# Aggregating neighbours on one core: second-pass steps regrouped over the slots, and half of the first pass's spreading given to GpSimd

## The chip, the cores and the metric

One core of one Trainium2 chip runs the kernel. The metric is the device time of the program in microseconds; each kernel is executed many times and the median is compared. A profile is one execution taken with the hardware profiler.

## The reference

```python
num_nodes, num_edges, dim = 4096, 65536, 128
for i in range(len(edge_index_src)):
    output[edge_index_dst[i]] += node_features[edge_index_src[i]]
```

Every edge adds the 128 features of its source node to its destination node. Source and destination are random integers below 4096, the features are float32, and the output is 4096 x 128 float32.

## The kernel before

**The idea.** Nodes are numbered in 32 blocks of 128. The sum over edges becomes matrix products, if the edges are first sorted by source block and by destination block. The kernel sorts them on the chip in two passes. A pass gives each edge a rank (a count of the earlier edges in its bucket), builds a one-hot permutation matrix from the ranks, and moves the edges with a matmul on TensorE. At the end each slot (one of 32) builds, for its destination block, count matrices between blocks of nodes, and multiplies the features with them.

**Engines and order.** The order of the instructions on every engine is written out by hand: each engine runs its own queue in the order in which the code emits it, and waits on semaphores for the others. The letters in the code are V (VectorE, DVE in the profile), S (ScalarE, ACT), G (GpSimd, POOL) and PE (TensorE).

**First pass, six quads (`for q in range(NQ)`).** A quad is four columns of edges. For quad q, `oh1s` (V) compares the destination blocks with an iota that lies in PSUM, `counts` (PE and S) makes the ranks, and `spread1` (line 262) multiplies the one-hot by two keys. It fills the tile `v1[q]`, whose two halves k=0 (key `ka`, the node codes) and k=1 (key `kb`, the source blocks) are one V instruction each, 128 x 2816. `move1` then builds the permutation `p` on V (line 201, the helper `onehot`) and runs the matmuls `psm` (line 286) with `v1` as the moving operand. `v1` has two buffers, tags A0 and A1, so quad q+1's tile is free when quad q-1's matmuls have been done. While quads 2 to 5 are moved, `beside` counts group 0 of the second pass: `buckets0` (V), a product `vc` on G (line 361), and `ranks0`. `clear` (line 149) zeroes the permutation tiles `p2a` and `p2c` with four GpSimd memsets each. `x_part` (lines 186 and 190) splits the features in two parts, on S and G.

**Second pass, groups 0 to 5 with 4, 4, 4, 4, 8, 8 columns (`pass2`).** Each group is a list of steps; a step is a V part, a PE part and a part for two slots later. The steps of a group of four are: `buckets4` (line 596) with its `payloads` on G (line 535, six products) and the column sums; `sums_to_each` (V) with `counts_ranks` (PE, S, line 622 and on); two pairs of `permutations` (V, four one-hots of line 201 into `p2a` or `p2c`) and `permuted` (PE, line 581). After the second pair of a quad of columns, `quad_keys` makes the keys `slo` and `dlo` (line 412, V). A group of eight has: `buckets` (line 520), 32 short compares on V, one for each source block, then `before_all` (PE, line 528); `running` (line 547), eleven dependent additions on V, whose results G multiplies in `masked` (line 552, twelve products), and behind them in G's queue twelve `payloads`; `ranks` (PE, line 560); four pairs. G's products are appended to a list and handed out by `little`, but on G they simply stand in that order.

**The slots.** Slot n issues on V: the keys that are due, `onehots(n+1)` (two instructions of 128 x 4096), then the V parts of the slot's steps. On PE it issues: the 32 matmuls of `blocks(n)` (`psa`, line 657) and the 16 of `product` for slot n-1 (`pso`, line 664) in two halves, then the PE parts of the steps. `onehots` has two buffers, so `onehots(n+1)` waits for the blocks of slot n-1. `STEPS` says which groups make a step in which slot:

```python
STEPS = {0: (1, 2), 1: (1,), 2: (2,), 3: (3,), 4: (2,), 5: (3, 2), 6: (4,), 7: (4,), 8: (3,),
         9: (3,), 10: (4,), 12: (4,), 13: (4,), 14: (5,), 15: (5,), 16: (4,), 17: (4,), 18: (5,),
         20: (5,), 21: (5,), 24: (5,), 25: (5,)}
```

Group 1's first two steps stand ahead of the loop, around `onehots(0)`. Slot 4's one-hots need the keys of group 1, slot 8's those of group 2, and so on; slots 16 to 23 use group 4, and slots 24 to 31 group 5.

Of the kernel before, what the change touches and what calls it, by code (L numbers as in the profile page):

```python
# [8 lines left out]
P = 128  # L9
# [5 lines left out]
OP = mybir.AluOpType  # L15
AX = mybir.AxisListType

NB = 32
NCH = 24
NJ = 22  # L20
NH = NCH // 2
NQ = NCH // 4
# [2 lines left out]
BIG = 4096.0  # L25
GROUPS = (4, 4, 4, 4, 8, 8)

STEPS = {0: (1, 2), 1: (1,), 2: (2,), 3: (3,), 4: (2,), 5: (3, 2), 6: (4,), 7: (4,), 8: (3,),
         9: (3,), 10: (4,), 12: (4,), 13: (4,), 14: (5,), 15: (5,), 16: (4,), 17: (4,), 18: (5,),
         20: (5,), 21: (5,), 24: (5,), 25: (5,)}  # L30


WIN = ((0, 7, 0, 64), (7, 14, 4, 100), (14, NJ, 20, P))
# [3 lines left out]
def kernel(  # L37
# [32 lines left out]
    with ExitStack() as fast:  # L70
        fast.enter_context(tc.manual_schedule())
        _fast(fast, tc, node_features, src32, dst32, out, ident, fmax, flag_i, T)
# [6 lines left out]
def _fast(ctx, tc, X, src32, dst32, out, ident, fmax, flag_i, T):  # L79
    nc = tc.nc  # L80
    V, S, G, PE = nc.vector, nc.scalar, nc.gpsimd, nc.tensor
# [62 lines left out]
    p2a = sb1.tile([P, 2, NCH, P], BF16, name="p2a")  # L144

    def clear(t):
        for i in range(2):
            for h in range(2):
                G.memset(t[:, i, h * NH:(h + 1) * NH, (1 - h) * 64:(2 - h) * 64], 0.0)


    NL = NJ * 4
# [3 lines left out]
    kb = sb1.tile([P, NQ, NL, 2], BF16, name="kb", tag="K1")  # L156
    ka = sb1.tile([P, NQ, NL, 2], U16, name="ka", tag="K2")
    kab = ka[:].bitcast(BF16)
# [24 lines left out]
    def x_part(i, v):  # L183
        blks = slice(i % 2 * BX, (i % 2 + 1) * BX)
        if v == 0:
            S.copy(out=xr[i // 2][:, blks, 0, :], in_=xf[i])  # L186
        else:
            for h in range(2):
                bs = slice(i % 2 * BX + h * BX // 2, i % 2 * BX + (h + 1) * BX // 2)
                G.tensor_tensor(out=xr[i // 2][:, bs, 1, :], op=OP.subtract,  # L190
                                in0=xf[i][:, h * BX // 2:(h + 1) * BX // 2],
                                in1=xr[i // 2][:, bs, 0, :])
# [3 lines left out]
    oh1, sums, rank1, v1 = {}, {}, {}, {}  # L196
# [9 lines left out]
    def oh1q(q):  # L206
        return oh1[q // 2][:, q % 2]

    def oh1s(q):

        if q % 2 == 0:
            oh1[q // 2] = sb1.tile([P, 2, NL, NB], BF16, name="oh1", tag=f"o{q // 2}")
        onehot(oh1q(q), kd[:, q], NL, NB)
        pst = ps.tile([P, 512], F32, name="pst", tag=("ps2", "pso")[q % 2], bufs=1)
        for j in range(NJ):
            PE.matmul(out=pst[:, j:j + 1],  # L216
                      lhsT=oh1q(q)[:, 4 * j:4 * j + 4, :].rearrange("p l b -> p (l b)"),
                      rhs=ones[:, :1], start=True, stop=True)
        sums[q] = pst
# [32 lines left out]
    def count(q, n=99):  # L252
        for _ in range(n):
            next(counting[q], None)
# [2 lines left out]

    def spread1(q):

        v1[q] = sb1.tile([P, NL, 2, NB], BF16, name="v1", tag=f"A{q % 2}")  # L260
        for k, key in ((0, kab), (1, kb[:])):
            V.tensor_tensor(  # L262
                out=v1[q][:, :, k, :].rearrange("p t (b k) -> p t b k", k=2),
                in0=oh1q(q).rearrange("p t (b k) -> p t b k", k=2),
                in1=key[:, q, :, None, :].to_broadcast([P, NL, NB // 2, 2]), op=OP.mult)


    def place(q):
# [7 lines left out]
    def move1(q, meanwhile):  # L276
        psm = ps.tile([P, 512], F32, name="psm", tag="misc", bufs=1)
        for l in range(4):
            t = p1[l // 2]
            n = len([j for j in range(NJ) if j * NCH + q * 4 + l < T])  # L280
            for j0, j1, m0, m1 in WIN:
                j1 = min(j1, n)
                onehot(t[:, l % 2, j0:j1, m0:m1], rank1[q][:, l, j0:j1], j1 - j0, m1 - m0, m0=m0)
            meanwhile(l)
            for j in range(n):
                PE.matmul(out=psm[:, l * 64:(l + 1) * 64], lhsT=t[:, l % 2, j, :],  # L286
                          rhs=v1[q][:, 4 * j + l].rearrange("p k b -> p (k b)"),
                          start=j == 0, stop=j == n - 1)
        pv = psm[:, :256].rearrange("p (l k b) -> p l k b", l=4, k=2)
        S.copy(out=sa[:, place(q), :], in_=pv[:, :, 0, :])  # L290
        S.copy(out=sbk[:, place(q), :], in_=pv[:, :, 1, :])
# [37 lines left out]
    x_part(2, 1)  # L329
    count(0)  # L330
    spread1(0)
    scan(2)
    count(1, 2)
# [1 line left out]
    count(1)  # L335
    x_part(3, 0)
    x_part(3, 1)
    clear(p2a)


    keys2 = {}
# [73 lines left out]
    def most_rank(g, r):  # L415
        V.tensor_reduce(out=fmax[:, g:g + 1], in_=r[:, :, :, 0], op=OP.max, axis=AX.XY)
# [39 lines left out]
    def during(q):  # L456

        def step(l):
            beside(q, l)
            if l == 0:  # L460
                if q + 2 < NQ and q == 0:
                    count(2, 2)
                return
            if l == 1:
                if q + 3 < NQ:
                    scan(q + 3)
            if q + 2 < NQ:
                count(q + 2, 2)
        return step

    for q in range(NQ):
        if q == NQ - 1:
            p2c = sb1.tile([P, 2, NCH, P], BF16, name="p2c", tag="o2")
            clear(p2c)
            p2b += [p2c[:, 0], p2c[:, 1]]
        move1(q, during(q))
        if q + 2 < NQ:
            count(q + 2)
        if q + 4 < NQ:
            oh1s(q + 4)  # L480
        if q + 1 < NQ:
            spread1(q + 1)
# [13 lines left out]
    def pass2(g):  # L496
# [9 lines left out]
        def flat2(t):  # L506
            return t.rearrange("p c i s k -> p c (i s k)")

        def tiles():
            at = -(g - 1) % 3  # L510
            tags = ("c0", "o1", "o0")
            T2["o"] = sb1.tile(shape, BF16, name="oh2", tag=tags[at])[:]
            T2["c"] = sb1.tile(shape, BF16, name="cum2", tag=tags[(at + 1) % 3])[:]
            T2["v"] = sb1.tile(shape, BF16, name="v2", tag="F" if g % 2 == 0 else "c1")[:]

        def buckets():
            tiles()
            ds = slice(d0, d0 + gd)
            for s in range(NB):
                V.tensor_single_scalar(  # L520
                    out=T2["o"][:, :, :, s, :], scalar=float(s + 1), op=OP.is_equal,
                    in_=sbk[:, :, ds].rearrange("p c (i k) -> p c i k", k=kk))
# [17 lines left out]
                for c in range(0, NCH, 4):  # L540
                    small.append(((g, 1), lambda i=i, c=c: payload(i, slice(c, c + 4))))

        def running():
            cums = flat2(T2["c"]).rearrange("p (h c) w -> p h c w", h=2)
            ohs2 = flat2(T2["o"]).rearrange("p (h c) w -> p h c w", h=2)
            for c in range(1, NH):
                V.tensor_tensor(out=cums[:, :, c], in0=cums[:, :, c - 1], in1=ohs2[:, :, c - 1],  # L547
                                op=OP.add)

# [79 lines left out]
        pairs = []  # L629
# [5 lines left out]
        def both(*fs):  # L635
            return lambda: [f() for f in fs]

        if gd == 4:
            return [(both(buckets4, payloads), column_sums), (sums_to_each, counts_ranks)] + pairs
        return [(buckets, before_all), (both(running, masked, payloads),),  # L640
                (lambda: None, ranks)] + pairs


    def onehots(slot):

        oh = sb1.tile([P, 2, 4 * 8, P], BF16, name="oh", tag=f"t2{slot % 2}")
        at = slot % 4 * 32
        n = 16 if slot == 0 else 32
        for i in range(0, 32, n):
            for k, io in ((0, piotas), (1, piota)):  # L650
                onehot(oh[:, k, i:i + n], keys2[slot // 4][k][:, at + i:at + i + n], n, io=io)
        return oh
# [14 lines left out]
    def flag():  # L667
# [13 lines left out]
                               op=OP.not_equal)  # L681

    todo = [[]] + [pass2(g) for g in range(1, len(GROUPS))]

    def run(fs):
# [8 lines left out]
    for cs in done0:  # L694
        permute0((2, 3), cs)
    nvec, nmat = todo[1].pop(0)
    nvec1, nmat1 = todo[1].pop(0)
    nvec()
    ranks0(last0)
    permuted0((2, 3), done0, 0)  # L700
# [8 lines left out]
    nmat()  # L709
    put_keys(0, pa0)  # L710
    oh = onehots(0)
    nvec1()
    nmat1()
    most_rank(0, T0["r"])
    slots = NB
    prev, pso = None, None
# [1 line left out]
    for slot in range(slots):  # L718
        for f in late.pop(slot, ()):
            f()  # L720
        steps = [todo[g].pop(0) for g in STEPS.get(slot, ())]
        late[slot + 2] = [f for st in steps for f in st[2:]]
# [117 lines left out]
```

## Time and profile before

| what | value |
|---|---|
| median of 14 runs | 341.77 us (340.58 to 342.87) |
| the profiled execution | 341.12 us, its span 339.5 us |
| TensorE, weight loads | 292.4 us (86%), 245.3 us (72%) |
| VectorE | 286.0 us (84%) in 385 instructions |
| ScalarE | 195.2 us (58%) |
| GpSimd | 99.8 us (29%) in 109 instructions |
| mean granted TensorE clock | 0.951 |

The span runs from the first to the last instruction. The profile's page gives each engine's busy time, the span in 40 equal slices (8.5 us each) with the busy tenths of each engine, the chain of waits that ended last, and groups of instructions by line with the mean of one. Further views are the waits by engine, tables of stretches of time, and the timeline of one engine, in which equal neighbours are merged into one row. Starts in the timeline are in us from the span's start.

### The profile page before, as it was taken

The numbers are of one execution on the slowest core, as the hardware profiler recorded it, in microseconds if no ns is written. First come the engines' busy times: TensorE is split into PE (matmuls) and PEld (weight loads), VectorE is DVE, ScalarE is ACT, GpSimd is POOL, SyncE is SP. The second block draws the span as 40 slices with busy tenths as digits, with TensorE's granted clock in tenths as the row PEclk, the third lists the DMA queues.
The fourth block names the chain that finished last, engine by engine and source line by source line (L and its number), as shares of the span: only waits on it lengthen the run. The fifth ranks groups of instructions, "written<-read, shape, count | busy, mean of one in ns | idle before, by whom it ended". The sixth has DMA issues, their size and how long they took to land.

```text
span 339.5 us, 8887 instructions
## 1 busy us (share of the span) xinstructions
PE 292.4 (86%) x3880; PEld 245.3 (72%) x3880; DVE 286.0 (84%) x385; ACT 195.2 (58%) x395; POOL 99.8 (29%) x109
## 2 busy tenths in 40 slices
PE   0679798577389899899699999987999999999994
PEld 0468676576178688688588888866888888888883
DVE  4999999976969939958999899999989959958800
ACT  2766546211175856855555666572656676677761
POOL 6637021142507070003998000189910000000000
PEclk9999979967599999999979999997999999999998
DMA  8500000000000000100001001000100100100101
GB/s 240 131 2 5 2 3 2 2 4 2 1 2 3 2 0 2 33 3 0 2 2 31 2 3 33 0 2 0 34 2 2 33 0 2 33 0 3 33 2 31
DMA packets 8712, 5.82 MB, mean 17 GB/s; under 512 B 224, under 2 KB 8416, under 8 KB 8672
## 3 DMA queue, kind: packets, MB, share of 16 engines
q1 hardware_dynamic: 8528, 4.72, 5.1%
q10 hardware_dynamic: 144, 0.52, 0.6%
q8 instruction: 30, 0.49, 0.6%
q14 instruction: 10, 0.08, 0.1%
HBM read 3.15 MB, written 2.10 MB: 15 GB/s over the span
## 4 chain that ended last, share of the span: by engine, by line
PE 61%; DVE 26%; ACT 6%; issue 5%; DMA 2%; DVEq 0%; ACTq 0%
PE pso L664 30%; PE psa L657 15%; DVE oh L201 7%; PE ps L581 7%; DVE p L201 6%; DVE v L262 5%; DVE cum L547 5%; PE psr L560 3%; ACT cum L625 2%; DMA raw<-in_edge_index_dst_dram 2%; ACT a L659 1%; PE psx L305 1%; PE pst L390 1%; PE psm L286 1%; PE ps L404 1%
## 5 line engine op out<-in xcount | busy, mean ns | idle before, releaser
L659 ACT CAST a<-psa 128x512 fp32r<-128x512 f32 x256 | 131.6, 604 | 47.0 <-PE psa L657 46.9
L664 PE MATMUL pso<-a,xr 128*128 128x512 f32 x512 | 133.5, 403 | 0.0
L664 PEld LDWEIGHTS pso<-a,xr 128*128 128x128 f32 x512 | 91.6, 189 | 16.9
L201 DVE TENSOR_TENSOR oh<-psi,slo 128x4096 bf16<-128x4096 uint16 (+1 forms) x33 | 73.2, 2219 | 21.7 <-PE psa L657 21.3
L201 DVE TENSOR_TENSOR oh<-psi,dlo 128x4096 bf16<-128x4096 uint16 (+1 forms) x33 | 73.1, 2214 | 0.0
L657 PE MATMUL psa<-oh 128*128 128x128 bf16 x1024 | 70.1, 222 | 0.4
L657 PEld LDWEIGHTS <-oh 128*128 128x128 bf16 x1024 | 59.5, 99 | 12.0 <-issue 11.7
L535 POOL TENSOR_TENSOR v<-oh,sa 128x512 bf16<-128x512 bf16 x42 | 42.6, 1047 | 35.9 <-DVE oh L596 24.5
L552 POOL TENSOR_TENSOR cum<-cum,oh 128x512 bf16<-128x512 bf16 x24 | 29.5, 1249 | 68.0 <-DVE cum L547 34.6
L201 DVE TENSOR_TENSOR p<-psi,rank 128x448 bf16<-128x448 uint16 (+3 forms) x72 | 29.7, 470 | 0.0
L241 ACT ACTIVATE cum<-psc,minus 128x512 bf16<-128x512 f32 (+1 forms) x36 | 21.4, 655 | 11.6 <-PE psc L238 11.3
L286 PE MATMUL psm<-v,p 128*128 128x64 bf16 x512 | 21.1, 199 | 2.0 <-DVE p L201 1.8
L286 PEld LDWEIGHTS <-p 128*128 128x128 bf16 x512 | 18.9, 102 | 2.7 <-DVE p L201 2.4
L201 DVE TENSOR_TENSOR p2a<-psi,rank 128x768 bf16<-128x768 uint16 (+2 forms) x36 | 15.9, 502 | 2.6 <-ACT rank L565 2.6
L581 PE MATMUL ps<-v,p2a 128*128 128x32 bf16 x336 | 12.2, 195 | 6.2 <-DVE p2a L201 6.2
L547 DVE TENSOR_TENSOR cum<-cum,oh 128x512 bf16<-128x512 bf16 x22 | 16.1, 731 | 1.5 <-ACT cum L531 0.8
L625 ACT ACTIVATE cum<-psc,minus 128x512 bf16<-128x512 f32 x18 | 11.2, 693 | 10.6 <-PE psc L622 8.7
L581 PEld LDWEIGHTS <-p2a 128*128 128x128 bf16 x336 | 11.2, 103 | 8.3 <-DVE p2a L201 7.1
L201 DVE TENSOR_TENSOR p2c<-psi,rank 128x768 bf16<-128x768 uint16 (+2 forms) x36 | 15.8, 500 | 0.0
L190 POOL TENSOR_TENSOR xr<-xf,xr 128x512 fp32r<-128x512 f32 x8 | 11.8, 1496 | 13.2 <-ACT xr L186 13.2
L216 PE MATMUL pst<-ones,oh 128*128 128x1 bf16 x132 | 4.3, 164 | 12.2 <-DVE oh L201 12.2
L234 PE MATMUL psc<-oh,early 128*128 128x512 bf16 (+1 forms) x36 | 14.7, 408 | 0.0
(97 smaller groups left out, 290.1 us busy)
## 6 DMA issues: line engine op xcount, KB each, us to landing
xf<-in_node_features_dram SPq DMA_DIRECT2D x4, 512.0 KB, 7.5
out_dram<-rows SPq DMA_DIRECT2D x8, 256.0 KB, 2.3
raw<-in_edge_index_src_dram ACTq DMA_DIRECT2D x1, 512.0 KB, 5.0
raw<-in_edge_index_dst_dram SPq DMA_DIRECT2D x1, 512.0 KB, 5.2
```

Of the source, the lines that this page charges most:

```text
L201: V.tensor_tensor(out=dst.rearrange("p i (m k) -> p i m k", k=2), in0=io.rearrange("p i (m k) -> p i m k", k=2), in1=keys2[:, :, None, :]. ...
L241: S.activation(out=cum[:, :, 4 * j0:4 * (j0 + n)], func=RELU, bias=minus[:], in_=psc[:, :n * P].rearrange("p (t b) -> p b t", b=NB))
L262: V.tensor_tensor(out=v1[q][:, :, k, :].rearrange("p t (b k) -> p t b k", k=2), in0=oh1q(q).rearrange("p t (b k) -> p t b k", k=2), in1=ke ...
L286: PE.matmul(out=psm[:, l * 64:(l + 1) * 64], lhsT=t[:, l % 2, j, :], rhs=v1[q][:, 4 * j + l].rearrange("p k b -> p (k b)"), start=j == 0, ...
L535: G.tensor_tensor(out=T2["v"][:, cs, i], in0=T2["o"][:, cs, i], op=OP.mult, in1=sa[:, cs, None, ds].to_broadcast([P, cs.stop - cs.start, N ...
L547: V.tensor_tensor(out=cums[:, :, c], in0=cums[:, :, c - 1], in1=ohs2[:, :, c - 1], op=OP.add)
L552: small.append(((g, 0), lambda c=c: G.tensor_tensor(out=flat2(T2["c"])[:, c:c + 2], in0=flat2(T2["c"])[:, c:c + 2], in1=flat2(T2["o"])[:, ...
L581: PE.matmul(out=ps2[:, d % 4 * NB:(d % 4 + 1) * NB], lhsT=p2b[d % 4][:, c, :], rhs=T2["v"][:, c, d // kk, :, d % kk], start=c == 0, stop=c ...
L625: S.activation(out=flat2(T2["c"])[:, c0:c0 + 4].rearrange("p c w -> p (c w)"), in_=psc[:], func=RELU, bias=minus[:])
L657: PE.matmul(out=psa[:, i * P:(i + 1) * P], lhsT=oh[:, 0, 4 * k + i, :], rhs=oh[:, 1, 4 * k + i, :], start=True, stop=True)
L659: S.copy(out=a[:, k, :], in_=psa[:])
L664: PE.matmul(out=pso[:], lhsT=xr[s // 16][:, s % 16, v, :], rhs=a[:, k, :], start=s == 0 and v == 0, stop=s == NB - 1 and v == 1)
```

## The change

Three things are changed. First, `spread1` of quads 1 to 5 keeps only the half `ka` on VectorE; the half `kb` of quad q+1 is made by GpSimd in four pieces of 128 x 704, put into its queue at the start of quad q's move. `clear(p2a)` moves from ahead of the loop to behind the pieces of quad 2. Quad 0 is still spread by VectorE alone. Second, the second step of group 1 moves from ahead of the slots into slot 0. Third, a group of eight has ten steps and not seven: its 32 compares are made in two halves of 16, `before_all` is a step of its own, and `running` is made in two parts of five and six additions. `STEPS` is rewritten to spread these.

```diff
-STEPS = {0: (1, 2), 1: (1,), 2: (2,), 3: (3,), 4: (2,), 5: (3, 2), 6: (4,), 7: (4,), 8: (3,),
-         9: (3,), 10: (4,), 12: (4,), 13: (4,), 14: (5,), 15: (5,), 16: (4,), 17: (4,), 18: (5,),
-         20: (5,), 21: (5,), 24: (5,), 25: (5,)}
+STEPS = {0: (1, 2), 1: (1, 1), 2: (2, 3), 3: (4,), 4: (2, 3), 5: (2,), 6: (4, 4), 7: (4,),
+         8: (3, 4), 9: (3,), 10: (4, 5), 11: (5,), 12: (4,), 13: (4, 5), 14: (5,), 15: (5,),
+         16: (4,), 17: (4,), 18: (5,), 20: (5,), 21: (5,), 24: (5,), 25: (5,)}
...
     def spread1(q):
+        if q == 0:
+            new_v1(q)
+            times_key(V, q, 1, 0, NL)
+        times_key(V, q, 0, 0, NL)
+
+    def new_v1(q):
         v1[q] = sb1.tile([P, NL, 2, NB], BF16, name="v1", tag=f"A{q % 2}")
-        for k, key in ((0, kab), (1, kb[:])):
-            V.tensor_tensor(
-                out=v1[q][:, :, k, :].rearrange("p t (b k) -> p t b k", k=2),
-                in0=oh1q(q).rearrange("p t (b k) -> p t b k", k=2),
-                in1=key[:, q, :, None, :].to_broadcast([P, NL, NB // 2, 2]), op=OP.mult)
+
+    def times_key(e, q, k, t0, t1):
+        e.tensor_tensor(
+            out=v1[q][:, t0:t1, k, :].rearrange("p t (b k) -> p t b k", k=2),
+            in0=oh1q(q)[:, t0:t1].rearrange("p t (b k) -> p t b k", k=2),
+            in1=(kab, kb[:])[k][:, q, t0:t1, None, :].to_broadcast([P, t1 - t0, NB // 2, 2]),
+            op=OP.mult)
...
     x_part(3, 1)
-    clear(p2a)
...
     for q in range(NQ):
+        if q + 1 < NQ:
+
+            new_v1(q + 1)
+            for t0 in range(0, NL, NL // 4):
+                times_key(G, q + 1, 1, t0, t0 + NL // 4)
+        if q == 1:
+            clear(p2a)
...
-        def buckets():
-            tiles()
+        def buckets(h):
+            if h == 0:
+                tiles()
             ds = slice(d0, d0 + gd)
-            for s in range(NB):
+            for s in range(h * NB // 2, (h + 1) * NB // 2):
...
-        def running():
+        def running(c0, c1):
...
-            for c in range(1, NH):
+            for c in range(c0, c1):
...
-        return [(buckets, before_all), (both(running, masked, payloads),),
-                (lambda: None, ranks)] + pairs
+        wait = lambda: None
+        return [(lambda: buckets(0),), (lambda: buckets(1),), (wait, before_all),
+                (lambda: running(1, 6),),
+                (both(lambda: running(6, NH), masked, payloads),),
+                (wait, ranks)] + pairs
...
     nvec, nmat = todo[1].pop(0)
-    nvec1, nmat1 = todo[1].pop(0)
...
     oh = onehots(0)
-    nvec1()
-    nmat1()
     most_rank(0, T0["r"])
```

## The prediction

> **What bounds the kernel now.** I read the page's busy slices and its chain first, then a table of stretches, TensorE's waits, and the timelines of VectorE and GpSimd.
>
> ```profile
> DVE  4999999976969939958999899999989959958800
> ...
> PE 61%; DVE 26%; ACT 6%; issue 5%; DMA 2%; DVEq 0%; ACTq 0%
> ...
> 20.00:30.00 10.00, 8.18 (x170) 6.91 (x169) 10.00 (x17) 7.55 (x16) 4.38 (x4) 1.00 0.01 2
> ...
> 84.00:98.00 14.00, 7.39 (x94) 5.41 (x92) 11.33 (x12) 4.39 (x9) 5.13 (x6) 0.61 0.00 1
> ...
> 231.50:300.00 68.50, 68.50 (x806) 58.30 (x807) 60.56 (x51) 43.76 (x88) 15.97 (x16) 0.98 0.05 13
> ...
> PE ps L581 <- DVE p2a L201: 6.2, 2, 3.3
> ...
> PE psc L622 <- DVE sums L612: 5.8, 1, 5.8
> ```
>
> The stretches list PE, PEld, DVE, ACT, POOL, clock, DMA. The chain gives TensorE 61% and VectorE 26% of the span. From 14 to 68 us VectorE is full and sets the pace; between 84 and 98 us neither engine is full; from 98 us on TensorE is full, but for two holes of 3.3 us (first wait row), after the eleven additions of groups 4 and 5. So the change has three places to gain: VectorE's half `kb` in the first pass, the 5.8 us at the slots' start, and the two holes. What it costs shows only in the timelines:
>
> ```profile
> 27.31 3.88 POOL L190 TENSOR_TENSOR xr<-xf,xr 128x512 fp32r<-128x512 f32 x2 [5.62 <-ACT xr L186]
> ...
> 27.41 2.66 DVE L262 TENSOR_TENSOR v<-oh,ka 128x2816 bf16<-128x2816 bf16 x1
> ...
> 156.53 8.40 DVE L547 TENSOR_TENSOR cum<-cum,oh 128x512 bf16<-128x512 bf16 x11 [0.84 <-ACT cum L531]
> ...
> 173.73 12.11 POOL L535 TENSOR_TENSOR v<-oh,sa 128x512 bf16<-128x512 bf16 x12
> ...
> 181.75 4.25 DVE L412 TENSOR_SCALAR slo<-pa 128x256 uint16<-128x256 uint16 x1
> 185.92 0.28 DVE L412 TENSOR_SCALAR dlo<-pa 128x256 uint16<-128x256 uint16 x1
> ...
> 209.32 3.90 DVE L520 TENSOR_SCALAR oh<-sbk 128x192 bf16<-128x192 bf16 x32
> ```
>
> `ka` takes 1.61 us alone but 2.66 beside GpSimd's first product; `slo` takes 0.28 alone but 4.25 while the twelve payloads end (185.84). The one-hots of line 201, which read an iota in PSUM and one tile in SBUF, take 2.28 beside GpSimd and 2.28 without. So VectorE's products of two SBUF tiles and its compares and shifts wait for GpSimd, and GpSimd for them. At 27.41, 84.41 and 85.08 VectorE got in after one GpSimd instruction; at 181.75 only when GpSimd's queue was empty.
>
> The Trainium skill ("SBUF — State Buffer", SBUF: two separate sides) has one port pair for both, held for a whole instruction by whoever starts first. By that `slo` would have waited for one payload, 1.04 us, and not for four; the row shows more than the rule. It speaks against this change either way.
>
> **First pass.** VectorE loses five `kb` halves: 10.7 us for six (1788 ns each) less 1.61 for quad 0, so 9.1 us of a full engine. GpSimd gets 20 pieces of 704. The nearest row is the payload, with the same types and a second operand repeated along the free dimension: 1.01 us from start to start for 512. With memsets' 0.03 us of fixed cost a piece is 1.38. The masked product of plain operands, 1.12 for 512, would make it 1.53. No row of two inputs is cheaper than the payload's. I take 1.38, 5.5 us a quad. GpSimd's queue then holds, without a gap from 27.3 us on: two `x_part` products 2.5, 20 pieces 27.6, `clear(p2a)` 2.7, three `vc` 3.1, and five `ka` of VectorE that lock it out, 5 x 1.55 = 7.8. Sum 43.7, so quad 5's `kb` is ready at 71.0. Before, quad 5's matmuls began at 71.6, behind `ranks0`. VectorE itself would be at quad 5's permutation only 1 us earlier than before, since at each quad it waits for TensorE's matmuls, which wait for GpSimd's pieces (quad 1: ready at 36.7, needed at 31.2). And behind `kb` stand `vc`, `clear(p2c)` and another `vc`, 1.05 + 2.75 + 1.05: at 75.9 the last product for `permuted0`, which began at 75.95 before. So the 9.1 us come to nothing: I take 0; the range goes from -1 (VectorE's lead) to +3 us (20 pieces at 1.53). GpSimd becomes the bound here.
>
> By the Trainium skill ("GPSIMD Engine Reference", Elementwise — side-by-side cycle accounting), 2.6 cycles an element at 1.2 GHz, a piece would be an estimated 1.53 us and this term 3 us instead of 0.
>
> **Slots 0 to 6.** Before, TensorE waited 5.8 us for group 1's scans (90.88), did its ranks until 97.4, then blocks(0), `permuted` (1.5) and group 2's column sums; slot 1's blocks began at 102.34. Now blocks(0) fill the hole (88.5 to 92.5), but the scans are queued behind `onehots(1)`: 90.95 + 4.4 = 95.4. The ranks take 5.6 (115.12 to 120.73, full clock) to 6.5 (90.88 to 97.4, half), column sums 0.6. Slot 1 starts at 95.6 + 6.0 + 0.6 = 102.2, as before, but with 1.5 us of `permuted` still to do. That is +1.4 us, and it stays, because TensorE is full from there on. `buckets4` of group 3 and the first 16 compares of group 4 (1.9) come to slots where VectorE waits for TensorE anyway (5.1 us before 124.67). Slot 7 starts at 156.8 instead of 155.43.
>
> **Slots 7 to 10.** A slot of TensorE is 5.63 us (109.48 to 115.12), plus 1.52 for `permuted`, 2.53 for `before_all`, 2.67 for group 4's `ranks`, 0.39 where results are transposed. VectorE has 4.4 for two one-hots, 1.85 for four of `permutations`. The additions are 0.46 each, but 1.3 where GpSimd's masked product holds it. The eleven (8.4) become 3.15 + 4.45. Running sum: additions start 1.1 us after slot 7's start, at 157.9; to 161.05; onehots(9) to 165.45; permutations to 167.3; additions to 171.75; onehots(10) to 176.15; permutations. TensorE: slot 7 to 162.4, slot 8 to 168.1, `permuted` to 169.6, slot 9 to 175.6, and then it waits; the last permuted block ends 2.38 after the permutations start (169.25 to 171.63), at 178.5. Slot 10 started at 180.14 before. So the hole shrinks from 3.3 us (and 0.8 at half clock after it) to about 1.3: -3.0 here, -1.6 since the start.
>
> **Slots 10 to 13: what is late next.** Group 4's last addition ends at 171.75, 6.8 us later than before (164.93). Behind it GpSimd has 8.8 us of masked products (164.93 to 173.73) and 12.1 of payloads: they run from 180.6 to 192.7. VectorE now reaches the first 16 compares of group 5 at 182.4 (onehots(11) from 178.0). Before, these stood in slot 14 with GpSimd idle (row 209.32). If each waits for one payload of 1.04, the payloads, slowed a little, end at 193.2 and the other compares at 193.8; if all wait for the queue's end, it is 194.6. I take 194. Behind them on VectorE are group 3's keys (0.6) and onehots(12), 4.4: ready at 199.0. TensorE has done slots 10 and 11 at 178.5 + 5.63 + 2.67 + 5.63 = 192.5. It idles 6.5 us, and slot 12 starts at 199.1 instead of 194.1. It then runs some 3 us at half clock, as after the hole at 166.5 (16 `psa` 1.71 instead of 0.91).
>
> **Slots 12 to 19.** VectorE now leads: 16 compares to 200.9, onehots(13) to 205.3, permutations to 207.15, onehots(14) to 211.55, permutations to 213.4. TensorE, at half clock at first (+2), has slot 12 done at 206.7, `permuted` at 208.2, slot 13 at 214.2, `permuted` and `before_all` at 218.3: slot 14 starts. The additions start 1.1 later and end at 222.55; group 4's keys wait for a masked product (to 224.15); onehots(16) to 228.55, additions to 233.0, onehots(17) to 237.4; `permuted` ends 2.38 later, and slot 17 starts at 239.8 (233.43 before). With 6.02 and 1.52, slot 18 starts at 247.3 (241.69 before). The payloads of group 5 end at 233.0 + 8.8 + 12.1 = 253.9 and may hold slot 19's keys to there; onehots(20) is then ready at 258.6, before TensorE asks at 261.2. After that TensorE is full as before, and the delay stays. Sum of the second pass: 247.3 - 241.7 = +5.6 us; of it +1.4 by slot 7, -3.0 by slot 10, +6.6 by slot 12 and +0.6 after.
>
> **Total.** 341.12 + 0 + 5.6 = 346.7 us by the profiled execution; that lay 0.65 below the median of 341.77, so 347.4 as a median.
>
> **Rivals.** (1) *Faster: the short compares are not held.* No row shows line 520 beside a busy GpSimd; in both bursts (142.41, 209.32) it was idle. If they pass, VectorE is free at 184.3, the keys wait for two payloads (186.7), onehots(12) is ready at 191.1, before 192.5, and the 6.5 us are not there. The same sums give slot 18 at 238.2, -3.5 us: 338.3. It decides whether VectorE has left the compares by 187.5. Against it: three other lines with the same kind of instruction (164, 174, 412) all waited beside GpSimd. (2) *Slower still: the first pass is starved.* If `ka` waits as `slo` did at 181.75, until the queue is empty, then quad 2's waits to 42.2, quad 3's to 58.0, and quad 5's permutation begins at 73.6 instead of 67.6: +6, 353. If the pieces cost 1.53, it is +3, 350. Against it: at 27.41 `ka` got in after one. (3) *The steps hide entirely behind TensorE and nothing moves:* for it, VectorE's total only falls; but its order at slot 11 speaks against it.
>
> **How the numbers follow.** Forecast 347.4, chance 0.58, own range 345 to 350. Rival 1 0.24 (336.5 to 340), rival 2 0.15 (350 to 355), rival 3 0.03. The range from 338 to 352 takes in the forecast, most of rival 1 and the nearer half of rival 2. A difference of 0.2%, 0.7 us, is what can be told from none. Faster 0.24, same 0.03, slower 0.73.
>
> **What would show it.** Right: GpSimd without a gap from 27 to some 71 us, quad 1's `psm` waiting for POOL, and TensorE's slot 1 near 102; the compares of line 520's second burst mixed with or behind payloads; a wait of TensorE for `oh` of some 6 us near 193 to 199, with a half clock after it; the two waits for `p2a` down from 3.3. Wrong: a first pass that ends some 5 us earlier, or compares that run at 0.12 us each while the payloads run.

## The result, and the profile after

The changed kernel takes 347.47 us (median of 10 runs, 345.23 to 349.95) against 341.91 for the kernel before (47 runs). The ratio is 1.0168, 95% interval 1.0145 to 1.0191: it is slower by 5.6 us. The forecast was 347.4, so the sum came out within 0.1 us, but that is partly luck: two of its terms were off by 1.4 and 2.0 us in opposite directions, a third by less, and their errors cancel.

The profiled execution of after took 351.18 us (span 349.6), 3.7 above its median, with a mean granted clock of 0.926 where most other executions had 0.93 to 0.95, so its stages are read beside those of the slots alone (the second experiment below), whose profiled execution of 348.64 us lay at its median.

The page of after, busy tenths in 40 slices (8.7 us each) and the chain's shares by engine:

```profile
PE   0688899584689989899999399997999999999994
...
DVE  4999779969977739398999999899988978967800
...
POOL 6628999946060700003399400349920000000000
PEclk9999699985559999999999879997899999999999
...
PE 54%; DVE 27%; ACT 4%; issue 2%; POOL 2%; DVEq 0%; ACTq 0%; POOLq 0%
```

GpSimd is now full in slices 4 to 8 (26 to 70 us), as forecast, and VectorE has some room there (7 tenths in slices 5 and 6). TensorE's clock is at half in slices 10 to 12 (79.3 to 106.6 us by the clock records; in before 81.2 to 94.9). The 3 in TensorE's row is new: slice 23, 192 to 201 us. The waits of TensorE in after (total, times, longest) name it:

```profile
PE psa L675 <- DVE oh L201: 9.8, 2, 5.9
...
PE ps L596 <- DVE p2a L201: 2.3, 1, 2.3
PE psc L637 <- DVE sums L627: 2.3, 1, 2.3
PE psm L294 <- POOL v L269: 2.3, 3, 1.0
```

The two waits for `p2a` of 6.2 us together have become one of 2.3 and one of 0.7 for `p2c`, and the 5.8 for the scans 2.3. But 9.8 us of waits for the one-hots are new: 3.9 before slot 0 and 5.9 before slot 12. The second one, in the timelines of after for VectorE, GpSimd and TensorE:

```profile
185.46 11.03 DVE L535 TENSOR_SCALAR oh<-sbk 128x192 bf16<-128x192 bf16 x16
...
183.70 12.12 POOL L550 TENSOR_TENSOR v<-oh,sa 128x512 bf16<-128x512 bf16 x12
...
201.50 1.89 PE L675 MATMUL psa<-oh 128*128 128x128 bf16 x16 [5.87 <-DVE oh L201]
```

Sixteen compares, 1.98 us in the second burst (201.37, GpSimd idle), take 11.03 beside the payloads. In the trace the second to the eleventh take 1.10 us each, one payload apiece; when the payloads end at 195.82, the last five follow at 0.12. The payloads themselves are not slowed (12.12 for 12.11). Slot 12's one-hots stand behind in VectorE's queue, and TensorE stops for 5.87 us and restarts at half clock (1.89 for 16 `psa`).

The place where each slot's first `psa` starts, and what the prediction made of it:

| place | before | after | slots alone | change since the last row, after | the same, slots alone | predicted |
|---|---|---|---|---|---|---|
| last compare of group 0 | 78.48 | 77.22 | 78.78 | -1.3 | +0.3 | 0 |
| slot 7 | 155.5 | 160.2 | 158.7 | +5.9 | +2.8 | +1.4 |
| slot 10 | 180.0 | 181.6 | 180.1 | -3.1 | -3.1 | -3.0 |
| slot 12 | 193.9 | 201.5 | 200.2 | +6.0 | +6.2 | +6.6 |
| slot 18 | 241.5 | 251.6 | 249.1 | +2.5 | +1.3 | +0.6 |

### The profile page after: what moved, and what is told of

It reads as the page before. It is cut to its first block, busy times and chain, and to the rows that moved or that the text cites. A ratio compares the mean times of both kernels' runs of the same rounds, so it can differ in the third digit from the quotient of the medians.

```text
span 349.6 us, 8911 instructions
## 1 busy us (share of the span) xinstructions
PE 300.8 (86%) x3880; PEld 252.3 (72%) x3880; DVE 283.9 (81%) x380; ACT 195.7 (56%) x395; POOL 131.8 (38%) x129
## 3 DMA queue, kind: packets, MB, share of 16 engines
HBM read 3.15 MB, written 2.10 MB: 15 GB/s over the span
## 4 chain that ended last, share of the span: by engine, by line
PE 54%; DVE 27%; ACT 4%; issue 2%; POOL 2%; DVEq 0%; ACTq 0%; POOLq 0%
PE pso L682 25%; PE psa L675 12%; DVE oh L201 11%; PE ps L596 4%; DVE cum L562 4%; DVE p L201 3%; DVE oh L535 3%; PE psr L575 2%; ACT cum L640 2%; DVE v L269 2%; PE psb L543 2%; PE psm L294 1%; POOL v L550 1%; PE pst L397 1%; PE psx L313 1%
## 5 line engine op out<-in xcount | busy, mean ns | idle before, releaser
L682 PE MATMUL pso<-a,xr 128*128 128x512 f32 x512 | 136.7, 410 | 0.0
L682 PEld LDWEIGHTS pso<-a,xr 128*128 128x128 f32 x512 | 94.1, 194 | 17.6
L675 PE MATMUL psa<-oh 128*128 128x128 bf16 x1024 | 72.2, 227 | 10.2 <-DVE oh L201 9.8
L675 PEld LDWEIGHTS <-oh 128*128 128x128 bf16 x1024 | 61.5, 101 | 22.3 <-issue 11.8
L269 POOL TENSOR_TENSOR v<-oh,kb 128x704 bf16<-128x704 bf16 x20 | 32.3, 1648 | 0.0
L201 DVE TENSOR_TENSOR p<-psi,rank 128x448 bf16<-128x448 uint16 (+3 forms) x72 | 29.7, 473 | 0.0
L535 DVE TENSOR_SCALAR oh<-sbk 128x192 bf16<-128x192 bf16 x64 | 17.0, 354 | 3.2 <-PE psr L575 3.2
L562 DVE TENSOR_TENSOR cum<-cum,oh 128x512 bf16<-128x512 bf16 x22 | 14.4, 654 | 2.9 <-ACT cum L546 2.3
L238 PEld LDWEIGHTS <-sums 128*128 128x128 bf16 x126 | 11.8, 112 | 5.1 <-issue 2.5
L234 PE MATMUL psc<-oh,early 128*128 128x512 bf16 (+1 forms) x36 | 15.4, 427 | 0.0
L238 PE MATMUL psc<-identb,sums 128*128 128x128 bf16 x126 | 14.9, 246 | 0.0
```

The source lines that it names most:

```text
L201: V.tensor_tensor(out=dst.rearrange("p i (m k) -> p i m k", k=2), in0=io.rearrange("p i (m k) -> p i m k", k=2), in1=keys2[:, :, None, :]. ...
L238: PE.matmul(out=psc[:, (j - j0) * P:(j - j0 + 1) * P], lhsT=sums[q][:, j - 1:j].to_broadcast([P, P]), rhs=identb[:], start=False, stop=j = ...
L269: e.tensor_tensor(out=v1[q][:, t0:t1, k, :].rearrange("p t (b k) -> p t b k", k=2), in0=oh1q(q)[:, t0:t1].rearrange("p t (b k) -> p t b k" ...
L535: V.tensor_single_scalar(out=T2["o"][:, :, :, s, :], scalar=float(s + 1), op=OP.is_equal, in_=sbk[:, :, ds].rearrange("p c (i k) -> p c i ...
L675: PE.matmul(out=psa[:, i * P:(i + 1) * P], lhsT=oh[:, 0, 4 * k + i, :], rhs=oh[:, 1, 4 * k + i, :], start=True, stop=True)
L682: PE.matmul(out=pso[:], lhsT=xr[s // 16][:, s % 16, v, :], rhs=a[:, k, :], start=s == 0 and v == 0, stop=s == NB - 1 and v == 1)
```

## The experiments

The theory was the prediction's: the first pass is worth nothing, because GpSimd takes the place of VectorE; the regrouped slots lose before slot 12, because compares of group 5 are held by the payloads of group 4. Each time below is a median beside that of the kernel before on the same chip; "below after" is the difference to after's 347.47.

**The first-pass part alone.** The kernel before with `times_key` and the moved `clear`, its `STEPS` and groups unchanged:

```diff
 (in the kernel before)
+            for t0 in range(0, NL, NL // 4):
+                times_key(G, q + 1, 1, t0, t0 + NL // 4)
```

> The kernel before with the first-pass part alone (GpSimd makes kb of quads 1 to 5). If GpSimd's queue bounds the first pass, VectorE's 9.1 us come to about nothing: the last compare of group 0 came 1.3 us earlier in the changed kernel (77.2 for 78.5), so -1.3 us, 340.6. If the first pass were still bound by VectorE, -5 us or more. If the regrouped slots alone were to blame and the spread were a real gain of its own, the same -5.

Measured: 340.13 against 342.13, ratio 0.9933 (0.9907 to 0.996). The part is a gain of 2.0 us, where the prediction took 0 and the forecast above -1.3. Quad 5's matmuls, first in before, then in this run, and the pieces of quad 5 in GpSimd's timeline here:

```profile
71.60 1.28 PE L286 MATMUL psm<-v,p 128*128 128x64 bf16 x21
...
69.07 1.28 PE L294 MATMUL psm<-v,p 128*128 128x64 bf16 x21
...
62.33 6.75 POOL L269 TENSOR_TENSOR v<-oh,kb 128x704 bf16<-128x704 bf16 x4
```

The pieces end at 69.1, and the matmuls begin 2.5 us earlier than before.

**The slots alone.** The changed kernel with the first pass of before:

```diff
 (in the changed kernel)
-        times_key(V, q, 0, 0, NL)
+        for k, key in ((0, kab), (1, kb[:])):
+            V.tensor_tensor(...)
```

> The changed kernel with the first pass of before (both halves on VectorE): all that the regrouping of the slots does. If the loss is all in the slots: +7.0 us against the kernel before, 348.9. If GpSimd's pieces in the first pass were part of the loss (by a longer first pass, or by delays handed on): less than +5.6, 347 or lower.

Measured: 348.56 against 342.13, ratio 1.019 (1.0161 to 1.0218): the regrouped slots cost 6.4 us, near the 7.0 of the first forecast. With the -2.0 this makes +4.4; the whole change measured +5.6, and the intervals of the parts, some 1 us each way, leave that open.

**Group 5's compares after the payloads.** Only `STEPS` is changed, so that the compares of group 5 stand in slots 12 and 13, when group 4's payloads are done:

```diff
-         8: (3, 4), 9: (3,), 10: (4, 5), 11: (5,), 12: (4,), 13: (4, 5), 14: (5,), 15: (5,),
+         8: (3, 4), 9: (3,), 10: (4,), 12: (4, 5), 13: (4, 5, 5), 14: (5,), 15: (5,),
```

> The changed kernel with group 5's two halves of compares moved from slots 10 and 11 to 12 and 13, behind the payloads; GpSimd's queue is as in the changed kernel. If only the compares were held: slot 12 starts without a wait, 341 to 342. If the keys of group 3, which now come first to VectorE beside the payloads, are held to the end of the queue as in the kernel before (4.25 us for 0.28): they end near 195, and TensorE still waits some 5 us for its one-hots: 345 to 347. If the hold has no part in the loss: 347.5.

Measured: 339.15 against 342.19, ratio 0.9907 (0.9884 to 0.993), 8.3 us below after, and faster than before. VectorE and GpSimd in its timelines:

```profile
184.25 0.46 DVE L419 TENSOR_SCALAR slo<-pa 128x256 uint16<-128x256 uint16 x1
184.62 1.14 DVE L419 TENSOR_SCALAR dlo<-pa 128x256 uint16<-128x256 uint16 x1
...
198.82 2.00 DVE L535 TENSOR_SCALAR oh<-sbk 128x192 bf16<-128x192 bf16 x16
...
182.49 12.23 POOL L550 TENSOR_TENSOR v<-oh,sa 128x512 bf16<-128x512 bf16 x12
```

The 16 compares take 2.00, the wait before slot 12 is gone (slot 12 starts at 194.3 in a span of 339.8), and the keys were not held to the end of the queue, which the second forecast had feared. The 8.3 us are more than the 5.87 of the wait: the half clock behind it goes too, and slot 12 takes 7.1 us instead of 9.0.

**The same mechanism put into the kernel before.** If the hold is the cause, the kernel before must get it by moving group 5's 32 compares to slot 9, beside the payloads:

```diff
 (in the kernel before)
-         ... 6: (4,), 7: (4,), ... 9: (3,), 10: (4,), ... 14: (5,), 15: (5,)
+         ... 6: (4, 4), 7: (4,), ... 9: (3, 5), 10: (4,), ... 14: (5,), 15: (5,)
...
-        return [(buckets, before_all), (both(running, masked, payloads),),
+        return [(buckets,), (lambda: None, before_all), (both(running, masked, payloads),),
```

> The kernel before with one thing moved: group 5's 32 compares from slot 14 to slot 9, where the twelve payloads of group 4 run (its step is split, so that its matmuls stay in slot 14, and group 4's stays whole in slot 6). If a compare waits for one payload each: eight are held to 185.9, the others take 2.9, onehots(11) end at 193 for 188.4 wanted, so +4.5 to +5.5 us, 347. If compares of this size pass between payloads: no change, 342, or less, as slot 14 has less to do.

Measured: 348.05 against 342.19, ratio 1.0173 (1.0146 to 1.0199). Timelines of VectorE and GpSimd, and TensorE's waits:

```profile
178.56 11.32 DVE L520 TENSOR_SCALAR oh<-sbk 128x192 bf16<-128x192 bf16 x32
...
174.92 12.15 POOL L535 TENSOR_TENSOR v<-oh,sa 128x512 bf16<-128x512 bf16 x12
...
PE psa L657 <- DVE oh L201: 4.5, 1, 4.5
```

The wait and the half clock behind it (192.0 to 198.8 in the trace's clock records) come into a kernel that has no other part of the change, and with them 5.9 us. More work ahead of slot 11's one-hots is not the reason by itself: the 32 compares took 3.90 alone, so 7.4 of their 11.32 us are the hold, more than the 4.5 that TensorE waits.

**The payloads taken away from that place.** In the changed kernel the payloads of the groups of eight are put ahead of the additions and masked products in GpSimd's queue, so that none runs beside the compares:

```diff
-        return [(lambda: buckets(0),), (lambda: buckets(1),), (wait, before_all),
+        return [(lambda: buckets(0),), (lambda: buckets(1),), (payloads, before_all),
...
-                (both(lambda: running(6, NH), masked, payloads),),
+                (both(lambda: running(6, NH), masked),),
```

> The changed kernel with the twelve payload products of groups 4 and 5 put into GpSimd's queue ahead of the running sums and the masked products; the compares stay in their slots. Same work on each engine. If the compares of group 5 cost 6.5 us because they stand beside the payloads: that wait goes, 341 to 342, and each of the first 16 compares takes 0.12 us. If the loss is in the order of steps or the half clock: 347 to 348, as the changed kernel.

Measured: 343.31 against 342.13, ratio 1.0037 (1.0016 to 1.0058), 4.2 us below after. VectorE's timeline:

```profile
157.91 5.89 DVE L562 TENSOR_TENSOR cum<-cum,oh 128x512 bf16<-128x512 bf16 x5 [0.85 <-ACT cum L546]
...
184.94 2.00 DVE L535 TENSOR_SCALAR oh<-sbk 128x192 bf16<-128x192 bf16 x16
```

The compares are free again (2.00, at the same place in VectorE's queue), and TensorE does not wait before slot 12. The loss moved: the first five additions, 3.11 in after, take 5.89 beside the payloads, and later TensorE runs from 178.7 to 185.6 at half clock. From slot 7 to slot 11 it takes 34.5 us instead of 29.7. So only half of what the hold cost comes back.

**Group 1's second step ahead of the slots again.** The other term that was off, slots 0 to 6:

```diff
-STEPS = {0: (1, 2), 1: (1, 1), ...
+STEPS = {0: (1, 2), 1: (1,), ...
...
+    nvec1, nmat1 = todo[1].pop(0)
     oh = onehots(0)
+    nvec1()
+    nmat1()
```

> The changed kernel with group 1's second step put back ahead of the slots. If that move costs what the prediction said: 1.4 us less than the changed kernel, 346.1; if the half clock that the profile shows from 79.3 to 106.6 us comes from it, 3 to 5 us less, 343 to 344.5. If the loss is all in the held compares: no change, 347.5.

Measured: 343.72 against 342.13, ratio 1.0045 (1.0021 to 1.007), 3.8 us below after, the time of the second forecast. TensorE's timeline in after:

```profile
87.27 1.86 PE L675 MATMUL psa<-oh 128*128 128x128 bf16 x16 [3.91 <-DVE oh L201]
...
94.17 0.50 PE L637 MATMUL psc<-identb,sums 128*128 128x128 bf16 x3 [2.32 <-DVE sums L627]
...
99.61 2.72 PE L575 MATMUL psr<-cum,identb 128*128 128x96 bf16 x32 [0.78 <-ACT cum L640]
...
103.47 1.87 PE L675 MATMUL psa<-oh 128*128 128x128 bf16 x16
```

Blocks(0) did not fill the hole of 5.8 us; they cut it into 3.91 and 2.32. TensorE idles as long, and its work around the two waits runs at half clock: 1.86 for 16 `psa`, 2.72 for ranks that took 1.54 at 96.06 before. In after the half clock lasts from 79.3 to 106.6, here from 79.9 to 93.6, and slot 2 starts at 108.5 instead of 113.5.

But the half clock is not all of it. The slots alone have the same first slots, and their half clock there (82.0 to 92.2 and 95.6 to 99.0 us) is 13.7 us, no longer than in before. TensorE's timeline there:

```profile
88.84 1.86 PE L661 MATMUL psa<-oh 128*128 128x128 bf16 x16 [3.94 <-DVE oh L201]
...
95.74 0.50 PE L623 MATMUL psc<-identb,sums 128*128 128x128 bf16 x3 [2.85 <-DVE sums L613]
...
102.75 0.74 PE L606 MATMUL pst<-ones,oh 128*128 128x1 bf16 x24 [0.50 <-ACT rank L566]
103.35 1.05 PE L661 MATMUL psa<-oh 128*128 128x128 bf16 x16
```

Slot 1 starts at 103.35 (102.37 before), slot 2, behind one `permuted` more, at 112.0 (109.5), and slot 7 is 3.2 us late, 2.8 of it since the last compare of group 0. So much the move costs without a longer half clock; in the profile of after, where it lasts 27.3 us, 5.9.

**A version built on these, first try.** Group 1 ahead; group 4's additions in slots 6 and 7 instead of 7 and 8, so that its payloads come earlier; group 5's payloads right behind its compares (slots 11 and 12), its second additions in slot 18:

```diff
+STEPS = {0: (1, 2), 1: (1,), 2: (2, 3), 3: (4,), 4: (2, 3, 4), 5: (2, 4), 6: (4,), 7: (4,),
+         8: (3,), 9: (3,), 10: (4,), 11: (5,), 12: (4, 5), 13: (4, 5), 14: (5,), 16: (4,),
+         17: (4,), 18: (5,), 19: (5,), 20: (5,), 21: (5,), 24: (5,), 25: (5,)}
...
+        return [(lambda: buckets(0),), (both(lambda: buckets(1), payloads if g == 5 else wait),), (wait, before_all),
...
+                (both(lambda: running(6, NH), masked, wait if g == 5 else payloads),),
```

> The changed kernel with group 1's second step ahead of the slots again, group 4's compares, before_all and additions a slot or two earlier (additions in slots 6 and 7), group 5's compares in slots 11 and 12 with its payloads right behind them, and its second additions in slot 18. If hold and half clock explain the loss: faster than the kernel before, 335 to 338 (-2.0 of the first pass, -3 to -4 of the first hole). If the spreading of the steps costs by itself: 341 or more.

Measured: 339.69 against 342.19, ratio 0.9928 (0.9906 to 0.995). It missed: new waits took the place of those removed. TensorE's waits and VectorE's timeline:

```profile
PE psr L575 <- POOL cum L567: 4.1, 1, 4.1
...
180.47 4.24 DVE L419 TENSOR_SCALAR slo<-pa 128x256 uint16<-128x256 uint16 x1
```

Group 5's ranks stand in slot 19, one slot after the second additions, and wait for GpSimd's masked products (to 250.7).

**Where GpSimd bounds the first pass.** The kernel before with the first-pass part, but quad 1 left whole on VectorE, so that GpSimd has 16 pieces:

```diff
 (in the kernel before with the first-pass part)
-        if q == 0:
+        if q < 2:
             new_v1(q)
...
-        if q + 1 < NQ:
+        if 1 < q + 1 < NQ:
```

> The first-pass part alone, but with quad 1 left whole on VectorE, so that GpSimd makes kb of quads 2 to 5 only: 5.4 us less on GpSimd, 1.6 to 2.7 us more on VectorE. If GpSimd's queue is the bound of the first pass: faster than the first-pass part alone by 1 to 3 us, 337.5 to 339. If VectorE were the bound: slower than it by 1.6 us or more, 342.

Measured: 338.25 against 342.19, ratio 0.9884 (0.9859 to 0.991): 1.9 us below the run with 20 pieces. TensorE's waits for the tile `v`, and group 0's last compare, first with 20 pieces:

```profile
PE psm L294 <- POOL v L269: 3.4, 4, 1.0
...
75.88 0.42 DVE L363 TENSOR_TENSOR oh<-psi,sbk 128x512 bf16<-128x512 uint16 x1 [2.06 <-ACT sbk L299]
```

and with 16:

```profile
PE psm L294 <- DVE p L201: 0.2, 1, 0.2
...
74.49 0.42 DVE L363 TENSOR_TENSOR oh<-psi,sbk 128x512 bf16<-128x512 uint16 x1 [1.91 <-ACT sbk L299]
```

Less work for GpSimd and more for VectorE makes it faster: GpSimd is the bound with 20 pieces, as forecast, but not by so much that the gain is nothing.

**The two repairs of the slots together.** Group 1 ahead and group 5's compares in slots 12 and 13:

> The changed kernel with both edits: group 1's second step ahead of the slots again (alone: 343.72) and group 5's compares in slots 12 and 13 (alone: 339.15). The theory has two separate losses in the regrouped slots, some 4 us before slot 1 and some 8 us before slot 12, so together they should add up: 347.5 - 3.8 - 8.3 = 335.4, between 334.5 and 337; slot 1 near 101.4, slot 12 near 190, no wait of TensorE before slot 12. Rival: the time that group 1's step gives back only makes TensorE ask earlier for one-hots that VectorE has not got ready (the two second additions, the keys of slots 16 and 20), so a wait takes its place and the kernel stays at 338 to 339.5.

Measured: 337.25 against 342.11, ratio 0.9876 (0.9852 to 0.9899). Neither theory's number: the 335.4 of plain addition was not reached, nor did it stay at 338 to 339.5. Group 1's step is worth 1.9 us here and 3.8 above. One stretch of time (its bounds and length in us; then PE, PEld, DVE, ACT, POOL busy, and the clock), first of after, then of this kernel:

```profile
100.00:120.00 20.00, 19.50 (x256) 16.89 (x254) 13.47 (x19) 9.09 (x20) 6.76 (x8) 0.83 0.01 2
```

```profile
100.00:120.00 20.00, 17.92 (x239) 14.93 (x237) 18.05 (x28) 12.48 (x25) 11.68 (x12) 1.00 0.01 2
...
PE ps L596 <- DVE p2a L201: 3.0, 1, 3.0
```

TensorE is at full clock from 92.4 us on. Later the wait for `p2a` before slot 17, 3.0 us, is followed by 6.9 us at half clock (225.5 to 232.4), in the run with the compares alone by 3.4; that is some 1.1 us given back (slot 17 takes 9.5 instead of 8.4). The rest of the difference between 1.9 and 3.8 is not explained; with some 0.8 us of noise on each of the four medians there need not be one.

**All three.** The same with quad 1 left on VectorE:

> The same with the kb half of quad 1 back on VectorE, so that GpSimd spreads quads 2 to 5 only. In the kernel of before with the first-pass part alone that was worth 340.13 to 338.25, 1.9 us; the theory that GpSimd bounds the first pass expects the same here: 333.5, between 332.5 and 335.5, with the last compare of group 0 near 74.5 instead of 77. Rival: what is gained before the slots is lost to TensorE's half clock after its stop there, and it comes out within 1 us of the kernel without this edit.

Measured: 335.69 against 342.11, ratio 0.9814 (0.979 to 0.9838), 1.6 us below the run before it: the theory's 1.9 within the noise of some 0.8, with the last compare of group 0 at 74.46 instead of 76.05. It missed the 333.5 by what its parent had missed. This version beats both kernels: 6.4 us below before and 11.8 below after.

## Why the prediction was right, and where it was wrong

**The total** was right to 0.1 us and its main mechanism is shown: the hold of the compares makes a wait in after, disappears when they or the payloads move, and appears in the kernel before when they are put beside them.

**First pass: the term was mis-sized, -2.0 measured for 0.** Its reasoning stands in parts: GpSimd without a gap to 73.8 us (46.49 of 46.70 us busy from 27.3 to 74), quad 5's `kb` ready at 69.1 (forecast 71.0), the last `vc` product at 73.8 (75.9). The sum was 2 us too long in two terms: the pieces took 1.33 to 1.34 us from start to start instead of 1.38, and a GpSimd product that a `ka` breaks into took 2.65 to 2.76 instead of 1.27 to 1.37, so each `ka` cost GpSimd 1.39 and not 1.55. So quad 5's matmuls, which had begun at 71.60, could begin 2.5 us earlier, as they did in the run of this part alone; the forecast's 71.0 would have left 0.6. Rival 2 fell on the same rows: `ka` took 2.08 to 2.70 us, and in no quad did it wait until GpSimd's queue was empty. By the 2.6 cycles an element of the Trainium skill ("GPSIMD Engine Reference", Elementwise — side-by-side cycle accounting) a piece was estimated at 1.53 us; the runs show 1.38 at most where VectorE does not break in.

**Slots 0 to 6: mis-sized, +2.8 measured for +1.4.** The times at which work is ready were right: in the slots alone blocks(0) start at 88.84 (forecast 88.5) and the scans end TensorE's second wait at 95.74 (95.4). "Fill the hole" was too much said, since blocks(0) come some 4 us into it. What the term had too small is what TensorE does behind the scans: the ranks took 6.5 us (95.74 to 102.26), the upper end of its own 5.6 to 6.5, where it took 6.0, and it put at nothing a wait of 0.50 us for `rank` ahead of the column sums, once before slot 1 and once before slot 3 (at 123.93). Undoing the step is worth 3.8 us, and 1.9 without the held compares.

**Slots 7 to 10: right.** The additions took 3.11 and 4.39 (forecast 3.15 and 4.45), the wait of 2.92 us for `p2a` and the half clock behind it (170.0 to 173.4 us in before) went, a wait of 0.70 for `p2c` is left: -3.1 measured for -3.0.

**Slots 10 to 13: right.** Payloads from 183.7, the compares one per payload as the first of the two forms, TensorE's wait 5.9 for 6.5, slot 12 +6.0 for +6.6. Rival 1, compares not held, needed VectorE out of them by 187.5; it was out at 196.4. What the hold is worth in time is more than this row: 8.3 us when it is avoided.

**Slots 12 to 18: +1.3 measured for +0.6.** In the slots alone TensorE's wait before slot 17 is 2.35 us (3.30 before), slot 16 to 17 takes 9.9 (10.9 before) and slot 17 to 18 8.3 (8.2). The +2.5 in the profile of after is more by a longer half clock: slot 17 to 18 takes 9.7 there, with 6.8 us at half clock instead of 3.4. Rival 3, that nothing moves, fell with the slots.

So -2.0 for 0 in the first pass was paid back by the slots' start (+2.8 for +1.4) and by slots 12 to 18. A forecast that is right in its total by such a sum is no proof of its terms; the parts run one by one are.

## What to carry to other kernels

Before a row of short VectorE instructions is moved, look at what GpSimd runs at the new place: here 16 compares of 0.12 us became 11 us, since ten of them waited for a GpSimd product of 1.0 us each, and the work queued behind paid for it. Before a piece of TensorE work is put into a hole, ask when it is ready: here it came 4 us into the hole and divided it, and TensorE idled as long as before. And when a full engine is relieved, the next bound can be found by giving a part back: one quad returned to VectorE was worth another 1.9 us.

## What the runs showed of the hardware

**Two forms of the hold.** Compares beside payloads take turns with them (1.10 us each, payloads unslowed). The keys `slo` beside the same twelve payloads are held to the end of GpSimd's queue in before (4.25 at 181.75), in after at slot 19 and in the first try above; in after:

```profile
252.34 3.87 DVE L419 TENSOR_SCALAR slo<-pa 128x256 uint16<-128x256 uint16 x1
```

But with the compares later (184.25), `slo` took 0.46 and `dlo` 1.14: turns again. Over all twelve traces the place in the queue separates the two: `slo` that began during the second payload of six or twelve took 0.45 to 0.76 us (15 times), `slo` that began during the eighth or ninth of twelve 3.87 to 4.27 (14 times). The compares, which in after begin during the second, take turns up to the last. By the Trainium skill ("SBUF — State Buffer", SBUF: two separate sides) whoever starts first holds the shared ports for one whole instruction; the turns agree with that, the 3.87 to 4.27 us, in which three or four payloads run from start to end, do not. Why the place decides is open.

**The half clock comes in equal pieces.** In the clock records of all these runs the stretches at half clock inside the span last 3.4 us or a multiple: 6.8, 10.2, 13.7, 17.1, 20.5, 27.3. So the half clock behind a stop of TensorE comes in steps: the same wait of 2.35 us before slot 17 is followed by 3.4 us of it in the slots alone and by 6.8 in after.
